# Hybrid block on one core: the second third's token tiles turned between the first block's products, four slots for the gated recurrence's results, and a later mark for the attention's first loads

## The chip, the cores and the metric

The kernel runs on 1 core of a Trainium2 chip. The metric is the device time of one execution in microseconds (us); less is better. The time before is the median of three runs. A profiled execution, taken apart from those runs, gives the trace.

## The reference

`reference.py` computes one layer of a streaming encoder on x (1 x 2048 x 1024, float32), with 16 learned meta tokens put ahead of the 2048 (T = 2064 tokens) and dropped at the end. Cut to what matters:

```python
h = concat(meta, x)
p = rms_norm(h, g_pre) @ W_in               # 1024 -> 512 + 1544 + 1024 columns, three head groups
a = rg_lru(p_a)                             # conv of 4 taps, gates, h_t = a_t h_(t-1) + b_t, times gelu(y); width 256
b = forgetting_attention(p_b)               # 8 heads of 64, causal softmax(q k / 8 + c_i - c_j) v, c = cumsum(log sigmoid(f))
c = rwkv7(p_c)                              # 4 heads of 64, state S_t = S (diag(w) - kk (kk a)^T) + v k^T, o_t = S_t r_t
h = h + rms_norm(concat(a, b, c) @ W_out, g_post)
g, v = causal_dwconv3(rms_norm(h, f_pre) @ W_up)      # 1024 -> 2 x 2816
h = h + rms_norm((gelu(g) * v) @ W_down, f_post)
```

The attention's f is 8 columns of p, one forget gate for each head.

## The kernel before, in words

**Products.** Each float32 operand is split into a rounded high part and the rest (xh, xl for tokens, wh, wl for weights), and a product is three matmuls: high by high, low by high, high by low (`mm3`, and L193 to L195 in the input projection). The tile names in the profile follow that: `psp` is the PSUM tile of an input column, `psf` that of the forget gate, `pst` that of a transpose.

**The input projection** runs in three thirds ("parts") of the tokens, and each part in two blocks of 128-token tiles: tiles 0 to 3 and 4 to 6, 7 to 9 and 10 to 12, 13 and 14, 15 and 16. Blocks are 400 and 384, 384 and 384, 256 and 256 tokens long. `w_in_norm` (L207) takes a part's tiles: it loads a tile (`token_load`), takes the mean square on ACT (L124), the power on POOL (L128) and scales on DVE (L148); then PE turns it in two halves of four 128x128 transposes (L161, `pst`), ACT writes the high part (L167) and DVE the low part (L168, `xl`). `norm_transpose` takes a tile from `core.held` if one lies there, and loads it otherwise. `w_in_part` then makes the forget gate (`w_in_gate`: L335 on xh, L336 on xl) and 24 weight columns of 128 ("c" for RWKV, "a" for the gated recurrence, k, v, q), each on both blocks. In part 0 the weights come from the input, are split and kept in DRAM (scr_wk); in parts 1 and 2 wh and wl are loaded from there (L260). In part 0 the second block's tiles are left unturned at first and are turned after the first two columns' products on the first block; the two columns' weights are loaded ahead. In parts 1 and 2 all tiles are turned, then the gate is made on both blocks, then the columns follow.

**Beside it.** A list of generators, `Beside`, is advanced 1.25 steps for each step of the projection. It holds `recurrences`: the forget gate's sums, the RWKV recurrence in blocks of 256 tokens (three for each part) and, behind each, `lru_block`, the gated recurrence (RG-LRU) on the same 256 tokens. The RWKV block makes its pair products on PE (L1232 from rwrav and rwbk, L1237, in PSUM tiles `rps`), masks them on DVE (L1241), sends triangles through DRAM (L1255, L1260), inverts them row by row on DVE (MEMSET L1282, L1288 over rwia and rwitmp), and then runs small 32x32 products on PE (L1317) with DVE steps between (L1340, L1347). `lru_block` works in two halves of 128 rows: a load of its input from DRAM (L1550, rwlraw), the first step on ACT (L1557, into the tile rwlu), three on DVE (L1559), two products for the gates, L1567 to L1591 on DVE and ACT, and the store of rwlu (L1592, to scr_mix). The tile rwlu has two slots: the third half waits until the first half's store has read its slot.

**The order of the work** on an engine is the order in which the program issues it, with some instructions held behind a named other one (`issue_after`) and the pools' slots deciding what waits. Each engine runs its queue in order. The attention (`Attn.run`) begins when the projection's last part is nearly done: the loads of its first heads' k and q (L605, L632) are placed in SP's queue behind `core.settled`, and its first memsets on DVE behind `core.parted`. Both marks are set in the main loop when the count of the last part's columns reaches `SETTLED` = 17. SP issues nearly all DMAs of the kernel, in order.

The rest of the kernel is the attention, W_out, and the feed-forward network (`psu`, `uw`, `psd`), most of the span; the diff does not touch it.

Of the kernel before, what the change touches and what calls it, by code (L numbers as in the profile page):

```python
# [18 lines left out]
P = 128  # L19
D = 1024  # L20
KD = D // P
META = 16
# [185 lines left out]
def w_in_norm(core, pools, psum, x, meta, gain, part):  # L208
    blocks = []
    for b, tl in enumerate(w_in_tokens(part)):  # L210
        t0 = tl[0][0]
        n = sum(r for _, r in tl)
        hi = pools["xn"].tile([P, KD, n], F32R, tag=f"xh{b}", name=core.n("xh"))
        apart = b == 1 and part < 2
        lo = pools["x1" if apart else "xn"].tile([P, KD, n], F32R, tag=f"xl{b}", name=core.n("xl"))
        blocks.append((t0, n, tl, hi, lo))

    def tile(block, s, rows):
        t0, _, _, hi, lo = block
        src = meta if s < META else x[s - META : s - META + rows, :]  # L220
        late = part == 1 and (s, rows) not in blocks[0][2][:2]
        after = (lambda: core.tc.issue_after(core.rounded.ins)) if late else nullcontext
        norm_transpose(core, pools, psum, src, rows, gain, [(hi, lo, s - t0, 0, rows)], after)

    core.unturned = []
    for block in blocks:
        for s, rows in block[2]:
            if part == 0 and block is blocks[1]:
                core.unturned.append((block, s, rows))
            else:  # L230
                tile(block, s, rows)
    core.turn_tile = lambda: tile(*core.unturned.pop(0))
    return blocks


def w_in_kept(scr, c0):

    return scr["wk"][c0 // P]
# [76 lines left out]
def w_in_gate(core, pools, psum, w_in, blocks, scr, part):  # L315

    nc = core.nc
    c0 = 2048
    home, tag = ("w", "wh") if part else ("us", "us")
    w = pools[home].tile([P, KD, P], F32R, tag=tag, name=core.n("fw"))  # L320
    flat, kept = w[:].rearrange("p k c -> p (k c)").bitcast(F32), w_in_kept(scr, 3 * D)[0]
    if part == 0:
        raw = pools["st"].tile([P, KD, 8], F32, tag="stv", name=core.n("fraw"))
        nc.sync.dma_start(raw[:], w_in[:, c0 : c0 + 8].rearrange("(k p) c -> p k c", p=P))
        nc.vector.memset(w[:].bitcast(F32), 0.0)
        nc.scalar.activation(w[:, :, 0:8], raw[:], AF.Copy)
        nc.vector.tensor_tensor(w[:, :, 32:40], raw[:], w[:, :, 0:8], op=ALU.subtract)
        nc.sync.dma_start(kept, flat)
    else:
        nc.sync.dma_start(flat, kept)  # L330

    def products(t0, n, tl, hi, lo):
        ps = psum.tile([P, 512], F32, tag="mm", name=core.n("psf"))
        for k in range(KD):
            nc.tensor.matmul(ps[:, :n], w[:, k], hi[:, k], start=k == 0, stop=False)  # L335
            nc.tensor.matmul(ps[:, :n], w[:, k], lo[:, k], start=False, stop=k == KD - 1)  # L336
        a = pools["st"].tile([8, 400], F32, tag="sth", name=core.n("fa"))
        nc.scalar.activation(a[:, :n], ps[32:40, :n], AF.Copy)
        o = pools["st"].tile([8, 400], F32, tag="stl", name=core.n("fo"))
        nc.vector.tensor_tensor(o[:, :n], ps[0:8, :n], a[:, :n], op=ALU.add)  # L340
        nc.sync.dma_start(scr["f"][:, t0 : t0 + n], o[:, :n])

    return products


def w_in_part(core, pools, psum, w_in, blocks, scr, part):
    gate = w_in_gate(core, pools, psum, w_in, blocks, scr, part)
    units = [("c", 2056 + P * i) for i in range(8)] + [("a", P * i) for i in range(4)]
    units += [(s, c + P * i) for s, c in (("k", 1024), ("v", 1536), ("q", 512)) for i in range(4)]
    waiting = [None]  # L350

    def step(*args):

        after = w_in_step(core, pools, psum, *args, scr)
        if waiting[0]:
            waiting[0]()
        waiting[0] = after

    if part == 0:
        raws = pools["rp"].tile([P, 2, KD, P], F32, tag="rw_e", name=core.n("raw"))  # L360
        firsts = [
            (w_in_weights(core, pools, w_in, c0, scr, part, raws[:, i], i > 0), kind, c0)
            for i, (kind, c0) in enumerate(units[:2])
        ]
        for i, block in enumerate(blocks):
            gate(*block)
            yield i > 0
            for w, kind, c0 in firsts:
                step(w, block, kind, c0)
                if i == 0:  # L370
                    core.turn_tile()
                yield i > 0
            while core.unturned:
                core.turn_tile()
        del units[:2]
    else:
        for block in blocks:
            gate(*block)
        yield False
        yield True  # L380

    for kind, c0 in units[:-2]:
        w = w_in_weights(core, pools, w_in, c0, scr, part)
        for block in blocks:
            step(w, block, kind, c0)
            yield block is blocks[-1]

    last = [(w_in_weights(core, pools, w_in, c0, scr, part), kind, c0) for kind, c0 in units[-2:]]
    for block in blocks:
        for w, kind, c0 in last:  # L390
            step(w, block, kind, c0)
            yield kind == "q" and c0 == last[-1][2]
# [1143 lines left out]
def lru_block(core, R, scr, k, b):  # L1536

    nc = core.nc
    t0 = max(0, Rwkv.start(b))
    n = min(T, Rwkv.start(b + 1)) - t0  # L1540
    c0 = PAD + t0
    tt = nc.vector.tensor_tensor
    stt = nc.vector.scalar_tensor_tensor

    def tl(s):
        return R.t([P, 256], s, bufs=2 if s == "lu" else 1)[:, :n]

    def raw(row, a):
        t = R.t([P, 260], "lraw", bufs=2)[:, : c0 + n - a]
        nc.sync.dma_start(t, scr["p"][row : row + P, a : c0 + n])  # L1550
        return t

    for p in range(2):
        pc = slice(p, p + 1)
        x = raw(P * p, c0 - 3)
        u, r, g, al = (tl("l" + s) for s in ("u", "r", "g", "a"))
        nc.scalar.activation(u, x[:, 3:], AF.Identity, scale=k["conv_w"][:, 6 + p : 7 + p], bias=k["conv_b"][:, pc])  # L1557
        for i in range(3):
            stt(u, x[:, i : n + i], k["conv_w"][:, 2 * i + p : 2 * i + p + 1], u, op0=ALU.mult, op1=ALU.add)  # L1559


        ps = R.pe()
        pa, px = ps[:, :n], ps[:, 256 : 256 + n]
        nc.tensor.matmul(pa, k["ga_w"][:, p], u, start=True, stop=True)
        nc.tensor.matmul(px, k["gx_w"][:, p], u, start=True, stop=True)
        nc.scalar.activation(r, pa, AF.Abs, bias=k["ga_b"][:, pc])
        nc.vector.tensor_scalar(al, pa, k["ga_b"][:, pc], 0.0, op0=ALU.add, op1=ALU.min)  # L1567
        nc.scalar.activation(g, px, AF.Tanh, scale=0.5, bias=k["rate"][:, 2, pc])
        nc.scalar.activation(r, r, AF.Tanh, scale=0.5)
        nc.scalar.activation(al, al, AF.Exp)  # L1570
        stt(r, r, 1.0, al, op0=ALU.add, op1=ALU.mult)
        stt(g, g, 1.0, u, op0=ALU.add, op1=ALU.mult)
        yield
        nc.scalar.activation(al, r, AF.Exp, scale=k["rate"][:, 0, pc])
        nc.scalar.activation(r, r, AF.Tanh, scale=k["rate"][:, 1, pc])

        tt(u, al, al, op=ALU.mult)
        stt(r, u, 1.0, r, op0=ALU.add, op1=ALU.mult)
        nc.vector.tensor_scalar(r, r, 1e-34, None, op0=ALU.max)
        nc.scalar.activation(r, r, AF.Sqrt)  # L1580
        stt(g, g, 0.5, r, op0=ALU.mult, op1=ALU.mult)
        nc.vector.tensor_tensor_scan(u, al, g, k["h"][:, pc], op0=ALU.mult, op1=ALU.add)
        nc.vector.tensor_copy(k["h"][:, pc], u[:, n - 1 : n])

        ya, y = raw(2 * P + P * p, c0), r
        nc.scalar.activation(y, ya, AF.Square)
        nc.vector.tensor_scalar(y, y, 0.044715, 1.0, op0=ALU.mult, op1=ALU.add)
        tt(y, y, ya, op=ALU.mult)
        nc.scalar.activation(y, y, AF.Tanh, scale=0.7978845608028654)
        stt(y, y, 1.0, ya, op0=ALU.add, op1=ALU.mult)  # L1590
        stt(u, u, 0.5, y, op0=ALU.mult, op1=ALU.mult)  # L1591
        nc.sync.dma_start(scr["mix"][P * p : P * p + P, t0 : t0 + n], u)  # L1592
        yield
# [558 lines left out]


READY = 13
SETTLED = 17
PACE = 1.25

WIDE = (0, 5)
# [379 lines left out]
```

## Time and profile before

| what | value |
|---|---|
| three runs, us | 2938.65, 2940.53, 2941.93 |
| median, us | 2940.53 |
| profiled execution, us | 2949.89 |
| its span, us | 2948.2 |
| PE busy | 96% of the span, 18854 matmuls |
| PEld (weight loads, beside PE) | 83% |
| DVE, ACT, POOL busy | 68%, 51%, 44% |
| mean granted clock of PE | 0.979 |
| DMA, mean over the span | 180 GB/s |

The page of the profile gives the busy time of each engine (PE: TensorE's matmuls, PEld: its weight loads, DVE: VectorE, ACT: ScalarE, POOL: GpSimd; SPq is the queue of SyncE, which issues DMAs) and the span in 40 slices of 73.7 us, with the clock that PE was granted in tenths. The other views are answers from the trace: a timeline lists instructions by start, with the idle time ahead of them and what ended it in brackets; a table of windows gives the busy time and granted clock between two points; the list of waits groups the idle time of an engine by what released it. A line number L1232 is that of the kernel before.

### The profile page before, as it was taken

To read this page: it belongs to the slowest core of one execution; us is meant where nothing else is said; L and a number is where in the kernel's file an instruction comes from. 1 tells how busy PE (TensorE), PEld (TensorE's weight loads), DVE (VectorE), ACT (ScalarE), POOL (GpSimd) and SP (SyncE) were. 2 spreads that over 40 slices of the span, in tenths; PEclk is the share of its full clock that TensorE was granted. 3 is DMA by queue.
4 is the path that set the end of the run, shared out by engine and by line. 5 is a ranking of instruction groups with operands and counts; after the bars stand their busy time and mean duration, and the time that the engine had idled before them with its cause. 6 is when DMAs were issued, how large, how long until landed. Compare 5 with 4: busy or idle time off the path is not lost.

```text
span 2948.2 us, 53211 instructions
## 1 busy us (share of the span) xinstructions
PE 2844.4 (96%) x18854; PEld 2446.0 (83%) x18854; DVE 2006.8 (68%) x3839; ACT 1502.3 (51%) x2937; POOL 1297.5 (44%) x1572
## 2 busy tenths in 40 slices
PE   8999999999988889999999999999999999999998
PEld 8998989888965555666578999999999999787887
DVE  4357655665678875556656988887777787556766
ACT  3246452454436654545645656666666665324333
POOL 1001222222114667677624676456655444656443
PEclk9998999999978999999999999999999999999999
DMA  7775678577643348444264665577777765436453
GB/s 241 250 245 185 215 240 291 174 241 246 204 120 77 90 115 227 97 122 129 48 192 148 212 194 179 160 233 209 219 199 222 215 198 149 141 111 218 151 170 122
DMA packets 470343, 530.51 MB, mean 180 GB/s; under 512 B 86862, under 2 KB 356888, under 8 KB 468524
## 3 DMA queue, kind: packets, MB, share of 16 engines
q1 hardware_dynamic: 469308, 526.18, 59.1%
q8 instruction: 148, 2.42, 0.4%
q0 software_dynamic: 768, 0.93, 0.1%
q14 instruction: 119, 0.97, 0.1%
HBM read 368.07 MB, written 158.90 MB: 179 GB/s over the span
## 4 chain that ended last, share of the span: by engine, by line
PE 75%; DVE 8%; DMA 6%; ACT 5%; issue 3%; POOL 2%; SPq 1%; DVEq 0%; POOLq 0%; ACTq 0%
PE psu L193 9%; PE psu L194 9%; PE psu L195 9%; PE psp L194 4%; PE psp L195 4%; PE psp L193 4%; PE psd L193 4%; PE psd L194 4%; PE psd L195 4%; PE po L797 4%; PE sc L774 2%; PE mx L645 2%; PE pswo L193 2%; PE pswo L194 2%; PE pswo L195 2%
## 5 line engine op out<-in xcount | busy, mean ns | idle before, releaser
L194 PE MATMUL psu<-xo,uw 128*128 128x344 f32 x1848 | 591.5, 320 | 0.0
L193 PE MATMUL psu<-xo,uw 128*128 128x344 f32 x1848 | 586.4, 322 | 3.0 <-DVE vb L1972 2.1
L195 PE MATMUL psu<-xo,uw 128*128 128x344 f32 x1848 | 581.9, 320 | 0.4 <-DVE uw L1781 0.3
L193 PE MATMUL psp<-xh,wh 128*128 128x384 f32 (+2 forms) x1152 | 380.4, 330 | 0.5 <-DMA wh<-scr_wk 0.5
L194 PE MATMUL psp<-xl,wh 128*128 128x384 f32 (+2 forms) x1152 | 375.3, 326 | 0.0
L195 PE MATMUL psp<-xh,wl 128*128 128x384 f32 (+2 forms) x1152 | 373.9, 325 | 0.4 <-DMA wl<-scr_wk 0.4
L1781 DVE TENSOR_TENSOR uw<-uq,uw 128x512 fp32r<-128x512 f32 x341 | 318.2, 938 | 62.5 <-ACT uw L1780 56.5
L193 PEld LDWEIGHTS psu<-xo,uw 128*128 128x128 f32 x1848 | 345.9, 188 | 5.2 <-DVE vb L1972 3.7
L194 PEld LDWEIGHTS psu<-xo,uw 128*128 128x128 f32 x1848 | 347.2, 188 | 0.0
L195 PEld LDWEIGHTS psu<-xo,uw 128*128 128x128 f32 x1848 | 345.7, 188 | 1.1 <-DVE uw L1781 1.1
L1780 ACT ACTIVATE uw<-uq 128x512 fp32r<-128x512 f32 x462 | 287.9, 627 | 95.2 <-PE psu L195 42.0
L779 ACT ACTIVATE p<-sc,bias 128x512 f32<-128x512 f32 (+4 forms) x352 | 197.6, 590 | 168.5 <-PE sc L775 147.5
L650 DVE TENSOR_REDUCE mc<-mx 128x1 f32<-128x512 f32 (+5 forms) x352 | 190.8, 566 | 110.4 <-PE mx L645 78.1
L1920 DVE SCALAR_TENSOR_TENSOR uy<-psu,ffn_cols,uy 128x342 f32<-128x342 f32 (+1 forms) x390 | 220.5, 567 | 61.9 <-ACT uy L1918 60.4
L1928 POOL TENSOR_TENSOR uy<-uy,uy 128x342 f32<-128x342 f32 (+1 forms) x132 | 145.4, 1102 | 231.5 <-ACT uw L1780 56.6
L1781 POOL TENSOR_TENSOR uw<-uq,uw 128x512 fp32r<-128x512 f32 x121 | 183.6, 1518 | 131.9 <-ACT uw L1780 108.8
L193 PEld LDWEIGHTS psp<-xh,wh 128*128 128x128 f32 x1152 | 218.9, 190 | 6.4 <-issue 3.7
L194 PEld LDWEIGHTS psp<-xl,wh 128*128 128x128 f32 x1152 | 219.0, 190 | 5.6 <-issue 4.0
L195 PEld LDWEIGHTS psp<-xh,wl 128*128 128x128 f32 x1152 | 218.9, 190 | 4.9 <-issue 2.9
L818 POOL TENSOR_TENSOR acc<-acc,p 128x512 f32<-128x512 f32 (+3 forms) x186 | 196.1, 1057 | 56.3 <-DVE acc L818 26.8
L1781 DVE TENSOR_TENSOR fo<-u,fo 128x896 fp32r<-128x896 f32 x88 | 100.6, 1143 | 131.0 <-ACT fo L1780 130.5
L1780 ACT ACTIVATE fo<-u 128x896 fp32r<-128x896 f32 x88 | 81.2, 923 | 206.7 <-PE psd L195 118.8
(492 smaller groups left out, 6309.8 us busy)
## 6 DMA issues: line engine op xcount, KB each, us to landing
uq<-scr_us SPq DMA_DIRECT2D x220, 256.0 KB
uq<-in_ffn_up_dram SPq DMA_DIRECT2D x209, 256.0 KB
wh<-scr_wk SPq DMA_DIRECT2D x48, 512.0 KB
wl<-scr_wk SPq DMA_DIRECT2D x48, 512.0 KB
u<-scr_ff SPq DMA_DIRECT2D x88, 256.0 KB
scr_ff<-uy SPq DMA_DIRECT2D x110, 171.0 KB
raw<-in_w_in_dram SPq DMA_DIRECT2D x24, 512.0 KB
scr_wk<-wh SPq DMA_DIRECT2D x24, 512.0 KB
```

The source lines that it names most:

```text
L193: nc.tensor.matmul(out, ah, bh, start=first, stop=False, skip_group_check=more)
L194: nc.tensor.matmul(out, ah, bl, start=False, stop=False, skip_group_check=more)
L195: nc.tensor.matmul(out, al, bh, start=False, stop=last, skip_group_check=more)
L645: nc.tensor.matmul(ps[:rows, : e - a], q3[:, qo : qo + rows], k2[:, a:e], start=True, stop=not last)
L650: self.reduced = nc.vector.tensor_reduce(mc[:rows, i, ci : ci + 1], ps[:rows, : e - a], axis=AX.X, op=ALU.max)
L779: last = nc.scalar.activation(p[:rows, :w], ps[:rows, :w], AF.Exp, bias=bias[:rows, j : j + 1])
L797: mm = nc.tensor.matmul(po[at : at + 64, c0:n], v1[:rows, j], p[:rows, : n - c0], start=start and i < 2, stop=end and i + 2 >= len(group), ...
L818: eng.tensor_tensor(a, ps_[0][0][:rows, c0:n] if start and i == 1 else a, p[:rows, : n - c0], op=ALU.add)
L1780: core.nc.scalar.activation(hi, src, AF.Copy)
L1781: (eng or core.nc.vector).tensor_tensor(lo, src, hi, op=ALU.subtract)
L1920: core.conved = stt(y[:, :n], src[:, i : n + i], cw[:, 44 * i + cc : 44 * i + cc + 1], y[:, :n], op0=ALU.mult, op1=ALU.add)
L1928: core.pooled = nc.gpsimd.tensor_tensor(v[:, :n], g[:, :n], v[:, :n], op=ALU.mult)
```

## The change

It has three parts.

- *The second third's tiles.* In part 1, as in part 0 before, only the first block's three tiles are turned ahead; the second block's three tiles are loaded (into `core.held`) and are turned one by one between the products of the first two columns on the first block: one after each of these products, the last after both. The first two columns' weights are loaded ahead of the gate in part 1 too. The gate's weights of part 1 go to the `us` pool, as in part 0, and not to one of the two `wh` slots.
- *The gated recurrence's results.* The tile rwlu has four slots and not two.
- *The attention's first loads.* `SETTLED` is 21 and not 17: the loads of the first heads' k and q, and the attention's memsets, are placed four columns later.

```diff
@@ -222,13 +222,13 @@ def w_in_norm
-    core.unturned = []
-    for block in blocks:
-        for s, rows in block[2]:
-            if part == 0 and block is blocks[1]:
-                core.unturned.append((block, s, rows))
-            else:
-                tile(block, s, rows)
+    core.unturned = [(blocks[1], s, rows) for s, rows in blocks[1][2] if part < 2]
+    for s, rows in blocks[0][2]:
+        tile(blocks[0], s, rows)
+    if part == 1:
+        core.held = [token_load(core, pools, x[s - META : s - META + rows, :], rows) for _, s, rows in core.unturned]
+    for s, rows in blocks[1][2] if part == 2 else ():
+        tile(blocks[1], s, rows)
     core.turn_tile = lambda: tile(*core.unturned.pop(0))
@@ -316,7 +316,7 @@ def w_in_gate
-    home, tag = ("w", "wh") if part else ("us", "us")
+    home, tag = ("w", "wh") if part == 2 else ("us", "us")
@@ -358,8 +358,9 @@ def w_in_part
     if part == 0:
         raws = pools["rp"].tile([P, 2, KD, P], F32, tag="rw_e", name=core.n("raw"))
+    if part < 2:
         firsts = [
-            (w_in_weights(core, pools, w_in, c0, scr, part, raws[:, i], i > 0), kind, c0)
+            (w_in_weights(core, pools, w_in, c0, scr, part, *((raws[:, i], i > 0) if part == 0 else ())), kind, c0)
             for i, (kind, c0) in enumerate(units[:2])
         ]
@@ -367,7 +368,7 @@ def w_in_part
                 step(w, block, kind, c0)
-                if i == 0:
+                if core.unturned:
                     core.turn_tile()
@@ -1543,7 +1544,7 @@ def lru_block
-        return R.t([P, 256], s, bufs=2 if s == "lu" else 1)[:, :n]
+        return R.t([P, 256], s, bufs=4 if s == "lu" else 1)[:, :n]
@@ -2152,7 +2153,7 @@
-SETTLED = 17
+SETTLED = 21
```

The added line `if part < 2:` makes every line number behind it one higher in the change: L1232 is L1233 there, L1282 is L1283, and so on.

Three places in the engines' orders show what moved. The first is PE's order where the first third passes to the second. Before, the last of the second third's transposes (pst) come around the RWKV recurrence's pair products (rps) and then the gate (psf):

```order
L1178 MATMUL eps_2058<-ident,rwe_1982 128x128 x4
L161 MATMUL pst_3133<-ident,xt_3118 128x128
L161 MATMUL pst_3148<-ident,xt_3140 128x128 x4
L161 MATMUL pst_3155<-ident,xt_3140 128x128 x4
L161 MATMUL pst_3170<-ident,xt_3162 128x128 x4
L161 MATMUL pst_3177<-ident,xt_3162 128x128 x4
L1232 MATMUL rps_2138<-rwrav_2079,rwbk_2086 128x128
L1237 MATMUL rps_2139<-rwrav_2079,rwbk_2086 64x128 x2
...
L1209 MATMUL eps_2096<-rwsq_1994,bones 128x512
L161 MATMUL pst_3192<-ident,xt_3184 128x128 x4
...
L335 MATMUL psf_3230<-xh_3092,fw_3228 128x384
L336 MATMUL psf_3230<-xl_3093,fw_3228 128x384
```

The same place in the change, where psp_3293 is the first weight column on block 0 and xt_3140 block 0's last tile:

```order
L1179 MATMUL eps_2058<-ident,rwe_1982 128x128 x4
L161 MATMUL pst_3133<-ident,xt_3118 128x128 x2
L161 MATMUL pst_3148<-ident,xt_3140 128x128 x4
L161 MATMUL pst_3155<-ident,xt_3140 128x128 x4
L335 MATMUL psf_3178<-xh_3092,fw_3168 128x384
L336 MATMUL psf_3178<-xl_3093,fw_3168 128x384
...
L193 MATMUL psp_3293<-xh_3092,wh_3170 128x384
L194 MATMUL psp_3293<-xl_3093,wh_3170 128x384
L161 MATMUL pst_3327<-ident,xt_3162 128x128 x4
L161 MATMUL pst_3334<-ident,xt_3162 128x128 x4
```

The gate and the first column on block 0 have moved ahead of the pair products and of the second block's transposes.

The second is DVE's order a little later, around the recurrence's triangular inverse (rwia, rwitmp). Before, the low parts of the second block's last tiles (xl_3095) come ahead of the gated recurrence's steps (rwla, rwlg) and of the memset of the inverse:

```order
L168 TENSOR_TENSOR xl_3095<-pst_3214,xh_3094 128x4x128
L168 TENSOR_TENSOR xl_3095<-pst_3221,xh_3094 128x4x128
L1241 TENSOR_TENSOR rwsc_2136<-rps_2154,rmask 128x4x128
L1241 TENSOR_TENSOR rwsc_2136<-rps_2155,rmask 128x4x128
L1262 TENSOR_TENSOR rwbk_2086<-rwbk_2086,rwwc_2091 128x1024
L1567 TENSOR_SCALAR rwla_2928<-eps_2933,lru_cols 128x256
...
L1581 SCALAR_TENSOR_TENSOR rwlg_2927<-rwlg_2927,rwlr_2926 128x256
L1282 MEMSET rwia_2222 128x16
L1582 SCALAR_TENSOR_TENSOR rwlu_2925<-rwla_2928,lru_h,rwlg_2927 128x256
L1288 TENSOR_REDUCE rwix_2258<-rwitmp_2261 128x8
```

In the change, the rows around the same memset (L1283 there):

```order
L1592 SCALAR_TENSOR_TENSOR rwlu_2925<-rwlu_2925,rwlr_2926 128x256
L1283 MEMSET rwia_2222 128x16
L1289 TENSOR_REDUCE rwix_2258<-rwitmp_2261 128x8 x2
L168 TENSOR_TENSOR xl_3095<-pst_3409,xh_3094 128x4x128
L1289 TENSOR_REDUCE rwix_2258<-rwitmp_2261 128x8
L168 TENSOR_TENSOR xl_3095<-pst_3416,xh_3094 128x4x128
L1568 TENSOR_SCALAR rwla_3028<-eps_3033,lru_cols 128x256
L1289 TENSOR_REDUCE rwix_2258<-rwitmp_2261 128x8
L168 TENSOR_TENSOR xl_3095<-pst_3475,xh_3094 128x4x128
L168 TENSOR_TENSOR xl_3095<-pst_3482,xh_3094 128x4x128
```

The last four low parts have moved behind the memset, and steps of the inverse stand among them.

The third is SP's order late in the projection. Before, the attention's first loads (k, q) stand among the loads of the gated recurrence's input (rwlraw) and the store of its result (rwlu):

```order
L1805 DMA us_8822<-in_ffn_up_dram 128x2x128 x3
L605 DMA k_1402_11222<-scr_kh 64x1040
L632 DMA q_1404_11231<-scr_qh 64x512
L1550 DMA rwlraw_9576<-scr_p 128x256
L289 DMA scr_p<-stp_8355 128x256
L632 DMA q_1405_11235<-scr_qh 64x512
L605 DMA k_1402_11222<-scr_kh 64x1040
L632 DMA q_1403_11227<-scr_qh 64x512
L1550 DMA rwlraw_9626<-scr_p 128x259
L1592 DMA scr_mix<-rwlu_8192 128x256
```

In the change:

```order
L1806 DMA us_8822<-in_ffn_up_dram 128x2x128 x3
L1551 DMA rwlraw_9576<-scr_p 128x256
L289 DMA scr_p<-stp_8355 128x256
L1551 DMA rwlraw_9626<-scr_p 128x259
L1593 DMA scr_mix<-rwlu_8192 128x256
```

The five loads have moved further back in SP's queue.

## The prediction

> **What bounds the kernel now.** I read the page first, then the granted clock in windows of 20 us and of 1 us, then the PE timeline wherever one of these showed a hole, then the queues of the engines that PE waited for there.
>
> The page, parts 1 and 2:
>
> ```profile
> PE 2844.4 (96%) x18854; PEld 2446.0 (83%) x18854; DVE 2006.8 (68%) x3839; ACT 1502.3 (51%) x2937; POOL 1297.5 (44%) x1572
> ...
> PE   8999999999988889999999999999999999999998
> ...
> PEclk9998999999978999999999999999999999999999
> ```
>
> PE is the bound; time can be won only where it idles or where its clock was halved. The fourth slice of PEclk and the stretch of 8s at 850 to 1110 us show where.
>
> Six windows (columns: length, then busy us and count of PE, PEld, DVE, ACT, POOL, then PEclk, DMA share, GB/s):
>
> ```profile
> 267.64:280.98 13.34, 11.08 (x44) 7.62 (x44) 12.31 (x21) 5.73 (x13) 5.39 (x6) 0.50 0.68 223
> 284.28:287.58 3.30, 3.30 (x13) 2.90 (x10) 2.70 (x4) 1.07 (x3) 0.00 (x0) 0.52 0.10 11
> 288.00:291.80 3.80, 3.80 (x23) 3.80 (x22) 2.23 (x6) 1.57 (x4) 0.00 (x0) 1.00 0.11 12
> 625.88:629.20 3.32, 3.32 (x13) 2.96 (x13) 2.52 (x10) 2.77 (x5) 1.92 (x4) 0.50 1.06 363
> 728.40:738.20 9.80, 9.43 (x91) 8.71 (x91) 4.23 (x13) 2.73 (x6) 0.47 (x1) 0.50 0.67 220
> 854.00:888.00 34.00, 28.82 (x112) 19.92 (x114) 22.96 (x62) 12.52 (x29) 6.52 (x12) 0.51 0.64 148
> ```
>
> At a clock of 0.50 half of the busy time is lost: 5.5 + 1.6 = 7.1 us where the first third passes to the second, 4.7 us at 728, 14 us at 854. The third row is the full-speed rate: 23 matmuls in 3.80 us, 0.17 us each.
>
> PE's timeline (start, duration, line, tile, count, and in brackets the idle time before it with its releaser):
>
> ```profile
> 259.48 1.80 PE L161 MATMUL pst<-ident,xt 128*128 128x128 f32 x15
> ...
> 269.90 0.79 PE L1232 MATMUL rps<-rwrav,rwbk 64*128 64x128 f32 x2 [5.66 <-DVE rwbk L1200]
> ...
> 275.26 2.07 PE L1209 MATMUL eps<-rwsq,bones 128*128 128x512 f32 x2
> ...
> 281.21 0.48 PE L1232 MATMUL rps<-rwrav,rwbk 64*128 64x128 f32 x2
> ...
> 281.62 0.43 PE L1237 MATMUL rps<-rwrav,rwbk 64*64 64x128 f32 x4
> ...
> 281.99 0.48 PE L1232 MATMUL rps<-rwrav,rwbk 64*128 64x128 f32 x2
> ...
> 624.54 0.75 PE L1317 MATMUL rps<-rwxu,rwsc 32*32 32x32 f32 x64 [1.70 <-ACT rwsc L1270]
> ...
> 728.77 0.31 PE L1317 MATMUL rps<-rwxf,rwxu 32*32 32x32 f32 x2 [4.08 <-DVE rwxu L1347]
> ```
>
> A transpose costs 0.12 us, one L1232/L1237 pair 0.78 us at full clock. The holes of 5.66 and 4.08 us are each followed by the slow clock; even 1.70 us with 32x32 matmuls behind it brought one slow window.
>
> **The change part by part.** The sum is made against the profiled execution, 2949.89 us (span 2948.2). The three timed runs have a median of 2940.53, 9.4 us less; the same difference is applied to that. 0.2% is 5.9 us, about what a measurement of this kernel can tell from no change: faster means below 2934.6, slower above 2946.4.
>
> *First hole (259 to 294).* On PE, before, four of the second third's six tiles are transposed ahead of the first L1232 (L1233 in the change, whose line numbers are one higher from 361 on) and two behind it, before the gate. In the change, by the order shown above, the transposes of block 0, the gate and the first products on block 0 come first, and L1233 behind them. PE now waits for the low parts of block 0 instead of for rwbk. DVE's timeline from there:
>
> ```profile
> 261.65 1.87 DVE L168 TENSOR_TENSOR xl<-pst,xh 128x512 fp32r<-128x512 f32 x3
> ...
> 263.45 0.86 DVE L1190 SCALAR_TENSOR_TENSOR rwk<-rwk,rwkv_cols,eps 128x256 f32<-128x256 f32 x2
> ...
> 264.23 0.68 DVE L1198 TENSOR_TENSOR rwrav<-rwr,rwe 128x512 f32<-128x512 f32 x1
> ...
> 266.10 0.68 DVE L1192 SCALAR_TENSOR_TENSOR rwe<-rwe,rwk 128x512 f32<-128x512 f32 x1
> ```
>
> L336 needs the fifth L168 (third tile, first half). In the changed DVE order five L168 (0.61 each, 3.1), the two of L1190 (0.8) and three 512-column steps (0.68 less the 0.07 by which such rows overlap, 0.6 each, 1.8) come up to and with it: 261.65 + 5.7 = 267.4. PE has its 24 transposes and four L1178 (0.5) done at 259.48 + 3.4 = 262.9 and one L335 in between: idle 4.3 instead of 5.66, **−1.3**. The hole stays long enough for the slow clock. But gate, psp and transposes that use the whole array now follow, 7 us of them at half rate, where before the half-height L1232/L1237 came: one or two windows of 3.3 us, 1.7 to 3.3 lost, say 2.4, against 7.1: **−4.7**. The gate's weights come from a buffer free since the first third, so both wh buffers are free for the first two columns; that load's 0.5 MB at 30 to 40 us, and the first columns' arrival behind two token loads, I cost at 0 (a load takes 5 us, below, and PE reaches them 7 us after the last product); uncovered it is 0 to 2.
>
> *A new wait (294 to 300).* The last two tiles' transposes stand behind the first two columns on block 0. On DVE every L168 (xl, the low parts) stood ahead of MEMSET L1282, before; in the change the four of these two tiles stand behind it, with steps of the recurrence's triangular inverse (rwia, rwitmp: its rows return from DRAM) among them. What that MEMSET waits for, at this place and at 610 us:
>
> ```profile
> 284.07 1.29 DVE L1241 TENSOR_TENSOR rwsc<-rps,rmask 128x512 f32<-128x512 f32 x2 [1.97 <-PE rps L1232]
> ...
> 284.79 3.65 SPq L1255 DMA_DIRECT2D da<-rwsc  x8
> ...
> 296.68 0.17 DVE L1288 TENSOR_REDUCE rwix<-rwitmp 128x8 f32<-128x16 f32 x1
> ...
> 297.44 0.16 DVE L1288 TENSOR_REDUCE rwix<-rwitmp 128x8 f32<-128x24 f32 x1
> ...
> 612.78 1.87 SPq L1255 DMA_DIRECT2D da<-rwsc  x4
> ...
> 615.88 1.14 SPq L1260 DMA_DIRECT2D rwia<-da  x2
> ...
> 618.75 0.07 DVE L1282 MEMSET rwia<- 128x16 f32 x1 [4.45 <-DMA rwia<-da]
> ```
>
> From L1241's first half on: 0.7, eight issues 3.65, 1.2 until L1260 (614.65 to 615.88), 2.9 until the MEMSET may run: 8.4 us. In the change PE does, from 267.4 to the end of its second L1232 group, 35 gate and psp (6.0), 8 transposes (1.0), 8 pairs (6.2), L1209 (2.07 at half clock, 1.0) and the gated recurrence's two small products (estimated as much, 1.0), 15.2, plus the 1.7 to 3.3 of slow clock: 284.3 to 285.9, no earlier than now. So the MEMSET runs at 292.7 to 294.3; two L1288 steps follow (0.9 and 0.8 by their spacing), then three L168, one L1567 and two L1288 (2.7): the gate's first low product on block 1 at 297.1 to 298.7. PE reaches it 28 psp (4.8), 16 identity products (1.8), 16 transposes (1.9), the small products (1.0) and three matmuls (0.5) after that group, 10.0: 294.3 to 295.9. A wait of 2.8, **+2.8**; nothing stands behind it on PE that could run, in order as it is. From 0, should the DMA be back sooner, to 5. The slow clock may follow (1.7 to 3.3) or not: **+1.2**.
>
> *Four result slots and later loads (713 to 738).* The waits list has all of ACT's waits for a result's store; the rest is the worst of the six (SPq: DMA issues):
>
> ```profile
> ACT rwlu L1557 <- DMA scr_mix<-rwlu: 16.2, 6, 8.2
> 708.55 0.43 SPq L1550 DMA_DIRECT2D rwlraw<-scr_p  x1
> ...
> 713.69 0.60 ACT L1557 ACTIVATE rwlu<-rwlraw,lru_cols 128x256 f32<-128x256 f32 x1 [0.67 <-DMA rwlraw<-scr_p]
> ...
> 721.67 0.53 SPq L1550 DMA_DIRECT2D rwlraw<-scr_p  x1
> ...
> 722.51 0.33 SPq L1592 DMA_DIRECT2D scr_mix<-rwlu  x1
> ...
> 722.95 1.72 DVE L1340 TENSOR_TENSOR rwxf<-rps,rwxu 32x256 f32<-32x256 f32 x4
> ...
> 724.70 0.42 DVE L60 COPY stp<-psp 128x256 f32<-128x256 f32 x1
> ...
> 726.96 0.60 ACT L1557 ACTIVATE rwlu<-rwlraw,lru_cols 128x256 f32<-128x256 f32 x1 [8.18 <-DMA scr_mix<-rwlu]
> ...
> 727.60 0.48 DVE L1559 SCALAR_TENSOR_TENSOR rwlu<-rwlraw,lru_cols,rwlu 128x256 f32<-128x256 f32 x1 [2.17 <-ACT rwlu L1557]
> ...
> 728.30 0.88 DVE L1347 COPY rwxu<-rps 32x256 f32<-32x256 f32 x2
> ```
>
> ACT waits 8.18 us for a store issued at 722.51; DVE's L1559 waits for ACT, L1347 stands behind L1559, and PE's 4.08 us end with L1347. With four slots only the input is needed. In the change, the attention's five loads (k, q) are gone from ahead of the input, which is issued five issues of 0.53 and a little between them, some 3 us, sooner, at 718.5; with 5.1 us to land as at 708.55 it is there at 723.6 at the latest, before DVE needs it. DVE then runs on from 725.1 through L1559, L1288, L1559 (0.4, 0.2, 0.4) and half of L1347 (0.4): PE goes on at 726.6, not 728.77: **−2.1**. About 2 us of idle and the 32x32 products remain, as at 624.54; that the 4.7 us of slow clock go is even odds: **−2.4**. The other five waits on a store have no hole of PE beside them: 0. The loads moved later are wanted by the attention at about 850 (the sixth window), some 80 us after their new place, four columns on: 0, or up to 2 if they fall among its own.
>
> Sum: −1.3 − 4.7 + 2.8 + 1.2 − 2.1 − 2.4 = −6.5: 2943.4 for the profiled execution, **2934.0** for the median. What follows up to 1110 us keeps its work but in another mixture; taken as 0, with −6 (somewhat under half of the 14 us lost at 854) to +14 (as much again) as bounds.
>
> **A rule weighed.** The row of 625.88 shows the clock halved after 1.70 us of idle, and that of 267.64 shows it halved for four windows although PE was busy for 11.08 of 13.34 us. The Trainium skill (TensorE: Matmul & The Clock Gate, Part 1) says that the clock halves after an idle window of about 3.4 us and comes back after one busy window. Both rows disagree with that here, so I don't sum by it; it would make the sum the first rival's.
>
> **The rivals.** *The clock falls only after a hole as long as those of 5.66 and 4.08, and one window restores it, as in the rows of 284.28 and 625.88*: then 1.7 is lost at the first hole (−5.4), nothing at the new wait, and all 4.7 is won at 728: −1.3 − 5.4 + 2.8 − 2.1 − 4.7 = −10.7, 2929.8. Against it: the row of 624.54. By the Trainium skill's rule the same. 0.15.
>
> *The new wait does not come*, because the inverse's rows are back before PE is there: −10.5, 2930. Its bound by the 610 us rows speaks against it. 0.10.
>
> *No gain arrives*: the recurrence's chain, not PE, sets when the attention can run, and what PE wins it waits for at 850; in the change the last products run ahead of the recurrence: by its order 49 rather than 92 of them stand between the same two recurrence products ahead of the attention's first. For it: PE is at 0.85 of 34 us there. 2940.5. 0.18.
>
> *The attention starts worse*: more of the recurrence's chain of small products then stands beside it, each waiting for DVE, and the slow stretch of 854 lasts as long again. It decides if over half of that comes: +14 − 6.5 = +7.5, 2948. For it: that stretch has been slow for 34 us already, on holes of 2 to 3 us. Against it: its work is the same. 0.16.
>
> The change does put the tiles, slots and loads where it says, by the order; that it doesn't is no case.
>
> **How the numbers follow.** The forecast has 0.41, its own range is 2930 to 2939; two thirds of it lie below 2934.6. Faster: 0.27 + 0.15 + 0.10 = 0.52, rounded down to 0.51 for the second rival's upper end. Slower: 0.14 of the last rival. Same: the rest, 0.35. The range takes in the third rival whole, the low rivals with a little of the later stage's −6 (2922), and the last one up to 2947.
>
> **What would show it.** Right: an idle of 3.5 to 4.5 us before an L336 near 267, the clock back at full by 275; a wait of 2 to 4 us before a gate product near 297 with DVE L168 as its releaser, behind MEMSET L1283; no wait of ACT's L1558 on scr_mix; the hole near 720 to 728 halved. Wrong: the first hole gone or followed by 13 us of slow clock again; L168 of block 1 done before the MEMSET; a changed slow stretch at the attention's start that is larger than all of these.

## The result and the profile after

The change is slower: 2948.57 us, the median of 22 runs (2940.39 to 2959.38), against 2941.86 us for the kernel before, run 22 times beside it (2934.57 to 2956.53). The ratio is 1.0025, with an interval of 1.0014 to 1.0036, so some 7 us more. Two later runs of the same kernel gave 1.0028 (1.0016 to 1.0041) and 1.0049 (1.0030 to 1.0068).

Single executions of one kernel spread over some 20 us, and a profile shows one execution. The profiled one of before (2949.89 us) is among its longer ones, the first profiled one of the change (2940.39 us) is the shortest of 22. Two spans alone would tell the wrong sign here. So stages are compared below over several profiles: four executions of the change were profiled (spans 2938.7, 2945.3, 2957.7 and 2942.7 us).

The page of the first profile after, parts 1 and 2, for the lines shown of before:

```profile
PE 2828.0 (96%) x18854; PEld 2437.4 (83%) x18854; DVE 2002.6 (68%) x3839; ACT 1500.8 (51%) x2937; POOL 1301.8 (44%) x1572
...
PEclk9999999999979999999999999999999999999999
```

The slow slice at 221 to 295 us is gone from PEclk; the one at 850 us is still there.

PE's timeline at the first passage (start, duration, line, tile, count, idle before it and its releaser):

```profile
264.20 0.45 PE L335 MATMUL psf<-xh,fw 128*128 128x384 f32 x1 [0.60 <-DVE rwk L1191]
267.90 0.44 PE L336 MATMUL psf<-xl,fw 128*128 128x384 f32 x1 [3.26 <-DVE xl L168]
...
273.39 0.49 PE L1233 MATMUL rps<-rwrav,rwbk 64*128 64x128 f32 x2
...
295.63 0.44 PE L335 MATMUL psf<-xh,fw 128*128 128x384 f32 x1 [1.31 <-ACT xh L167]
...
296.79 0.44 PE L336 MATMUL psf<-xl,fw 128*128 128x384 f32 x1 [0.37 <-DVE xl L168]
```

The holes are 0.60 + 3.26 us, not 5.66, and the second ends with L168 at 267.90. The windows of the same profile (columns as in the prediction):

```profile
269.12:272.53 3.41, 3.41 (x15) 3.13 (x14) 3.40 (x7) 1.91 (x6) 1.49 (x2) 0.50 1.03 420
294.32:296.40 2.08, 0.77 (x3) 0.47 (x3) 2.08 (x7) 2.08 (x5) 0.74 (x3) 1.00 0.00 1
```

One window of 3.41 us at half clock follows the hole, where before there were 16.6 us of it. At the second place PE idles 1.3 of 2.08 us, and 0.37 us more before L336 at 296.79. DVE's timeline there:

```profile
293.15 0.07 DVE L1283 MEMSET rwia<- 128x16 f32 x1 [0.98 <-DMA rwia<-da]
...
294.27 0.69 DVE L168 TENSOR_TENSOR xl<-pst,xh 128x512 fp32r<-128x512 f32 x1
...
296.06 1.27 DVE L168 TENSOR_TENSOR xl<-pst,xh 128x512 fp32r<-128x512 f32 x2
```

The four L168 do stand behind the memset, which ran at 293.15 us.

Around 728 us, the windows from 700 to 745 us of before and of the change, one row each:

```profile
700.00:745.00 45.00, 39.56 (x528) 36.88 (x528) 25.10 (x72) 21.29 (x48) 16.48 (x28) 0.89 0.74 219
```

```profile
700.00:745.00 45.00, 42.58 (x620) 39.20 (x619) 27.00 (x80) 22.69 (x54) 14.56 (x26) 1.00 0.71 227
```

PE did 92 more matmuls in the same 45 us, at full clock. Of the hole of 4.08 us, 0.57 is left:

```profile
722.18 0.24 PE L1318 MATMUL rps<-rwxf,rwxu 32*32 32x32 f32 x2 [0.57 <-DVE rwxu L1348]
```

ACT waits for no store of rwlu any more; what is left of L1558's waits is its input:

```profile
ACT rwlu L1558 <- DMA rwlraw<-scr_p: 19.7, 9, 4.6
```

So both holes named in the prediction shrank, and the new wait is shorter than forecast. The time is lost behind the last weight column. Windows from the last product of a column to the first of W_out: before, and then, with the stretch ahead of it, the change's third profile (span 2957.7 us, an execution of 2959.45 us):

```profile
845.90:1157.40 311.50, 273.51 (x2230) 174.06 (x2229) 226.96 (x594) 172.91 (x370) 173.25 (x261) 0.88 0.50 129
```

```profile
0.00:836.10 836.10, 799.26 (x7035) 740.37 (x7035) 487.93 (x1219) 372.70 (x741) 155.02 (x268) 0.98 0.70 226
...
836.10:1166.30 330.20, 275.98 (x2306) 176.24 (x2305) 235.76 (x609) 175.27 (x375) 173.63 (x263) 0.87 0.48 121
```

The change has its columns done at 836.1 us, 9.8 us sooner than before, and then needs 330 us and not 311 us to reach W_out. In its other three profiles the columns end at 836.1, 836.0 and 837.6 us, and this stage takes 312, 320 and 314 us. What follows W_out's first product is the same in both within 2 us. Before was profiled once, in an execution 8 us above the median of its 22; if its spread is made in this stage, as that of the change is (last section), a usual execution of before takes some 303 us here, an estimate.

Why the stage is longer was not settled by these two traces; the experiments were made for that.

### The profile page after: what moved, and what is told of

Its sections match the earlier page's. It is cut to its first block, busy times and chain, and to the rows that moved or that the text cites. A ratio compares the mean times of both kernels' runs of the same rounds, so it can differ in the third digit from the quotient of the medians.

```text
span 2938.7 us, 53187 instructions
## 1 busy us (share of the span) xinstructions
PE 2828.0 (96%) x18854; PEld 2437.4 (83%) x18854; DVE 2002.6 (68%) x3839; ACT 1500.8 (51%) x2937; POOL 1301.8 (44%) x1572
## 4 chain that ended last, share of the span: by engine, by line
PE 72%; DVE 9%; DMA 6%; ACT 5%; issue 3%; POOL 3%; SPq 1%; DVEq 0%; POOLq 0%; ACTq 0%
PE psu L193 9%; PE psu L194 9%; PE psu L195 9%; PE po L798 4%; PE psd L193 4%; PE psd L194 4%; PE psd L195 4%; PE psp L193 4%; PE psp L195 4%; PE psp L194 4%; PE sc L775 2%; PE pswo L193 2%; PE pswo L194 2%; PE pswo L195 2%; PE mx L646 2%
```

## The experiments

The theories at the start: *(T)* the tiles cost, *(S)* the slots cost, *(L)* loads marked late reach the attention late, *(O)* the order on PE at the attention's start costs, by how the recurrence's rest lies among the attention's products. All times against the kernel before are ratios from runs on the same chip.

**Each part alone, and two together.** The tiles alone (the change with `bufs=2` and `SETTLED = 17`):

> Only the second third's tiles are turned between the first block's products; two result slots, mark at 17. By my sum of the four terms of the first passage (-1.3, -4.7, +2.8, +1.2) it is 2 us faster than the kernel before. If this part is what makes the change slower (it runs the recurrence beside other columns for the whole second third, so that its work stands in another place at every later hole), it is 5 us slower or more. If the cost lies in the later mark or in the slots, it is within 3 us of before.

1.0029 (1.0014 to 1.0043), slower by 8.6 us by the medians. Against my sum. The hole at 728 us is back, a row of PE's timeline in this kernel:

```profile
726.73 0.31 PE L1318 MATMUL rps<-rwxf,rwxu 32*32 32x32 f32 x2 [3.94 <-DVE rwxu L1348]
```

The slots alone:

```diff
-        return R.t([P, 256], s, bufs=2 if s == "lu" else 1)[:, :n]
+        return R.t([P, 256], s, bufs=4 if s == "lu" else 1)[:, :n]
```

> Only the four result slots. By my account the input of the fifth block's second half is then the last to arrive at 727 us, behind the attention's loads in SP's queue: hardly a gain, 0 to -2 us. If the slots let the gated recurrence run ahead and its steps then stand before the RWKV recurrence's on ACT and DVE, it is slower, by 3 us or more.

0.9992 (0.9978 to 1.0006). The hole of PE is halved with this alone, and the half-clock time there is mostly gone (granted clock 0.96 from 700 to 745 us, where before has 0.89):

```profile
732.69 0.24 PE L1317 MATMUL rps<-rwxf,rwxu 32*32 32x32 f32 x2 [2.04 <-DVE rwxu L1347]
```

What is left is the input, which comes last, as expected: in the list of ACT's waits of this kernel the stores are gone, and the longest wait for the input, 6.6 us, ends inside this hole, at 730.88 us:

```profile
ACT rwlu L1557 <- DMA rwlraw<-scr_p: 20.6, 10, 6.6
```

S falls.

The mark alone (`SETTLED = 21` in the kernel before):

> Only the mark of the attention's first loads and memsets at 21. By my account nothing is lost at the attention's start, and the store at 722 us leaves SP some 3 us sooner: 0 to -3 us. If the later loads reach the attention too late, or fall among its own, it is slower by 5 us or more, and PE waits at the first scores for a load of q or k.

0.9994 (0.9981 to 1.0006). From 700 to 745 us its granted clock is 0.99 and PE is busy for 42.0 us: the five loads out of SP's way were enough by themselves, although ACT still waits for the store here, 3.5 us and no longer 8.2. As the expectation's first branch; the hole in this kernel:

```profile
725.05 0.24 PE L1317 MATMUL rps<-rwxf,rwxu 32*32 32x32 f32 x2 [0.47 <-DVE rwxu L1347]
```

Tiles and slots, with the mark at 17:

> The change without the later mark. If the mark is what costs, it is at least 5 us faster than the whole change, so no slower than before. If the tiles or the slots cost, it stays about 7 us slower than before, like the whole change. By my sum: 2 to 4 us faster than before.

0.9992 (0.9978 to 1.0007), 2.7 us less by the medians. So what made tiles alone slow is not there with four slots, and the mark, harmless alone, made the change slow. The hole at 728 us is not what made them slow, for it is here too, with ACT waiting 8.4 us for its input:

```profile
729.90 0.24 PE L1318 MATMUL rps<-rwxf,rwxu 32*32 32x32 f32 x2 [3.92 <-DVE rwxu L1348]
```

The parts don't add up: 1.0029, 0.9992 and 0.9994 alone, 0.9992 for two, 1.0025 for all three. That speaks for something that all three move, which is O.

**Late loads or order.** The change once more, then three kernels in which loads and order part ways:

> The change once more, beside the next three on one chip, and with another profile. Both theories: 5 to 9 us slower than the kernel before. If its profile is a usual one, the time is lost between the last weight column (846 us before) and the end of the recurrence (about 1120), by 6 us or more against the 311 us of before; ahead of that it is no later than before.

1.0028 (1.0016 to 1.0041). Its profile, again the shortest of its executions, loses 9 us more in the stage than before; ahead of it it is 10 us sooner.

The change with only the loads late, the memsets at 17:

```diff
-                    if part == 2 and i == SETTLED:
-                        core.settled, core.parted = core.loaded.ins, core.split.ins
+                    if part == 2 and i == 21:
+                        core.settled = core.loaded.ins
+                    if part == 2 and i == 17:
+                        core.parted = core.split.ins
```

> The change, but only the loads of k and q have the later mark (21); the attention's memsets keep theirs (17). PE's order behind the attention's first product is then that of before but for 8 rows, and the loads are as late as in the change. If late loads are what costs: 5 to 9 us slower than before. If the order of PE's work in the attention's first 270 us is what costs: 1 to 5 us faster than before, like the tiles and slots without the mark.

0.9992 (0.9979 to 1.0004), like tiles and slots without the mark: L falls, O stands. The traces bear it out: at the attention's first scores PE waits for a load of q 2.0 to 2.6 us in the change's four profiles, and 2.2 us in before; before, then the change's first profile:

```profile
853.94 0.66 PE L774 MATMUL sc<-q,k 128*128 128x512 f32 x2 [2.18 <-DMA q<-scr_qh]
```

```profile
850.16 1.10 PE L775 MATMUL sc<-q,k 128*128 128x512 f32 x2 [1.99 <-DMA q<-scr_qh]
```

The same with 21 and 17 exchanged (only the memsets late):

> The change, but only the memsets have the later mark (21); the loads keep theirs (17). The recurrence's rest stands further back among the attention's products: its first hundreds of rps behind 119, 144, 206 and 304 products of the attention, like the change's 125, 152, 206 and 304, where before has 88, 114, 169 and 282. If late loads cost: 1 to 5 us faster than before. If the order costs: 4 to 9 us slower.

1.0005 (0.9993 to 1.0017): between the two branches, some 4 us over the run before it. It is neither the change's loss nor the gain. From the change it differs by the loads' mark alone, and it is 7 us faster by the medians; that mark moves PE's order as well (the table below has both), so how much is the order's was not told apart here.

The kernel before with `SETTLED = 16`:

> The kernel before with the mark at 16, one column earlier: neither the tiles nor the slots, and no load later than before. The recurrence's rest stands behind 119, 144, 206, 304, 347 and 522 products of the attention, as in the run before this one. If late loads cost: within 2 us of before. If the order costs: 5 to 10 us slower than before.

0.9995 (0.9984 to 1.0006). Here O, as I had put it, was wrong: the recurrence's hundreds stand behind nearly as many attention products as in the change, and it costs nothing. The count that matters had to be another one (below).

**The order put back.** The change with `SETTLED = 22`: every load and memset later still, PE's order behind the attention's first product that of before but for 8 rows.

> The change with the mark at 22 and not 21: the loads and the memsets come one column later still. PE's order behind the attention's first product is that of before but for 8 rows. If a late mark costs by itself: 6 to 10 us slower than before, like the change or worse. If PE's order at the attention's start costs: 1 to 5 us faster than before.

0.9971 (0.9952 to 0.9990), and with the run below 0.9978 (0.9967 to 0.9990). Nothing that the change adds is taken out, and by these ratios it is 6 to 9 us faster than before. Of the things that were told apart, only the order on PE (and on the engines that go with it) is left for the change's loss. Its median granted clock over the runs is 0.9835, where before has 0.981 and the change 0.9805 and 0.979: 0.0025 of 2940 us is 7 us, lost in some 15 us at half clock.

**The wait for the third keys.** All four profiles of the change have a wait of 7.4 to 8.5 us that before has with 2.1 us; the row in the list of waits of before, of the change's first profile and of its third:

```profile
PE mx L645 <- DMA k<-scr_cl: 2.1, 1, 2.1
```

```profile
PE mx L646 <- DMA k<-scr_cl: 7.5, 1, 7.5
```

```profile
PE mx L646 <- DMA k<-scr_cl: 8.5, 1, 8.5
```

The load stands behind the recurrence's last store in SP's queue. That store, moved to POOL's:

```diff
-        nc.sync.dma_start(
+        (nc.gpsimd if b == 8 else nc.sync).dma_start(
             self.scr["mix"][768:1024, t0 : t0 + n - a].rearrange("(p r) t -> r p t", r=P), fo[:, :, a:n]
```

> The change, with the RWKV recurrence's last store moved from SP's queue to POOL's; PE's order as in the change but for 12 rows. In both profiles of the change PE waits 7.5 us for k<-scr_cl near 1080 us, which stands behind that store in SP's queue; SP waits some 2 us there for the store. If the store's wait sets the hole: the hole shrinks by 2 us, and the time by 2 to 4 us against the change (3 to 7 us slower than before). If the hole comes from SP's whole order standing behind PE's: the hole stays over 6 us, and the time at 6 to 9 us above before.

1.0015 (0.9999 to 1.0031), and the hole is 5.4 us: the first branch, by 2 us of hole and about 3 us of time (the intervals of this and of the change overlap). What holds the load now, from the list of SP's waits between 1060 and 1092 us and from DVE's timeline in this kernel:

```profile
SPq L608 <- DVE k L568: 2.4, 1, 2.4
SPq L606 <- PE rps L1474: 1.7, 1, 1.7
```

```profile
1081.54 0.22 DVE L1482 TENSOR_TENSOR rwxu<-rwxu,rps 128x64 f32<-128x64 f32 x1
1081.79 2.81 DVE L568 CAST k<-ident 64x520 fp32r<-64x520 f32 x4
```

L606 waits for the recurrence's last product (L1474) and L568 follows its last DVE step (L1482) at once: the third key tile lies in memory that the recurrence holds to its end. So the attention's second half can't start before the recurrence has ended, wherever the store is.

**The tiles alone in another order** (`bufs=2`, `SETTLED = 22`):

> Only the tiles, with the mark at 22: another order behind the attention's first product (the recurrence's hundreds behind 88, 113, 158, 271, 306 and 466 products of the attention; the tiles alone with the mark at 17 have 88, 113, 153, 242, 279 and 414, before has 88, 114, 169, 282, 329 and 494). If the tiles themselves cost, it is 6 us or more slower than before, as the tiles alone were. If the order they came with cost, it is within 4 us of before.

1.0052 (1.0033 to 1.0072). Slower in this order too. By the expectation the tiles themselves cost with two slots; but this order isn't before's either, and no version of the tiles with two slots and before's order was found. That stays open.

**Side by side.** The change and the mark at 22 on one chip, and a fourth profile of the change:

> The change beside the same with the mark at 22, on one chip. Both earlier profiles of the change were its fastest executions. If the cost is the order at the attention's start, this kernel is 6 us or more slower than the next one, and a usual execution's profile loses it between the last weight column and the first product of W_out (846 to 1157 us before), in more slow clock and in a wait of over 5 us for k<-scr_cl; in the other stages it is within 3 us of the next kernel.

> The change with the mark at 22 once more. If the first run of it told the truth, it is 3 to 10 us faster than the kernel before and faster than the change on the same chip by 6 us or more. If that run was luck, it is within 2 us of before.

> One more profile of the change, for a usual execution: the wait for k<-scr_cl near 1080 us is over 5 us in it as in the other two, and the time is lost in the attention's start, not ahead of it.

1.0049 (1.0030 to 1.0068) for the change, 0.9978 (0.9967 to 0.9990) for the mark at 22: the version with the mark at 22 beats both kernels. The change's third profile is of a usual execution (2959.45 us, its median here 2960.01). The fourth is not: with 2944.42 us it is as fast as the median of before beside it (2944.32), though its wait for the third keys is 7.4 us. Two rows of the version with the mark at 22, to be held against those of the change above:

```profile
0.00:844.90 844.90, 806.74 (x7111) 745.71 (x7111) 490.06 (x1232) 375.14 (x745) 154.61 (x269) 0.98 0.69 224
...
844.90:1143.10 298.20, 263.93 (x2230) 168.79 (x2229) 226.77 (x594) 172.51 (x370) 172.28 (x260) 0.91 0.52 134
```

Its columns end 8.8 us later than the change's (the expectation had the other stages within 3 us), and it is at W_out 23.2 us sooner: 32 us between the two in one stage, 12 of them busy time of PE (275.98 against 263.93, at the lower clock and with 76 matmuls more) and 20 idle.

Where this comes from is seen in the place of one step: the last pair products (L1238) of the recurrence's last full block, behind which only a short block follows. First with the mark at 22, then in the change:

```profile
875.99 1.09 PE L1238 MATMUL rps<-rwrav,rwbk 64*64 64x128 f32 x16
```

```profile
891.98 1.97 PE L1238 MATMUL rps<-rwrav,rwbk 64*64 64x128 f32 x16
```

16 us later, although the columns were done 8.8 us sooner. Its end is 20.7 us later in these two profiles. With the mark at 22:

```profile
1063.74 0.33 PE L1474 MATMUL rps<-rwsg,g_up 128*128 128x64 f32 x2
...
1072.08 0.77 PE L646 MATMUL mx<-k,q 128*128 128x400 f32 x3 [1.81 <-DMA k<-scr_cl]
```

In the change:

```profile
1084.41 0.69 PE L1474 MATMUL rps<-rwsg,g_up 128*128 128x64 f32 x2
...
1094.57 1.31 PE L646 MATMUL mx<-k,q 128*128 128x400 f32 x3 [8.51 <-DMA k<-scr_cl]
```

Both have the second half's first product 8 to 10 us behind L1474; only, in the change PE is idle for 8.51 us of it.

Counted in the traces, for every profile (column products still to do behind the recurrence's L1394 near 839 us; attention products, that is mx, sc and po, ahead of the last full block's last row of L1238, and where that row starts; line numbers of the change; times in us):

| kernel | last column | column products left at L1394 | attention products ahead of that L1238 | at | last L1474 | first of W_out | ratio |
|---|---|---|---|---|---|---|---|
| before | 845.9 | 26 | 50 | 882 | 1077.9 | 1157.4 | 1 |
| slots | 847.4 | 28 | 50 | 884 | 1070.7 | 1148.9 | 0.9992 |
| tiles, slots | 844.7 | 28 | 50 | 882 | 1069.6 | 1149.6 | 0.9992 |
| loads late | 846.8 | 27 | 50 | 878 | 1063.5 | 1143.2 | 0.9992 |
| mark 22 | 846.4 | 21 | 50 | 883 | 1069.8 | 1148.9 | 0.9971 |
| mark 22 again | 844.9 | 21 | 50 | 876 | 1063.8 | 1143.1 | 0.9978 |
| before, mark 16 | 851.0 | 47 | 50 | 880 | 1072.0 | 1155.0 | 0.9995 |
| before, mark 21 | 845.1 | 9 | 98 | 887 | 1073.2 | 1156.1 | 0.9994 |
| memsets late | 847.6 | 11 | 77 | 887 | 1075.2 | 1155.0 | 1.0005 |
| the change | 836.1 | 0 | 110 | 890 | 1069.2 | 1148.2 | 1.0025 |
| the change again | 836.0 | 0 | 110 | 892 | 1077.1 | 1156.2 | 1.0028 |
| the change, third | 836.1 | 0 | 110 | 892 | 1084.7 | 1166.3 | 1.0049 |
| the change, fourth | 837.6 | 0 | 110 | 890 | 1070.9 | 1151.9 | |
| store on POOL | 839.1 | 0 | 110 | 893 | 1079.9 | 1156.6 | 1.0015 |
| tiles | 843.1 | 26 | 50 | 879 | 1066.4 | 1163.7 | 1.0029 |
| tiles, mark 22 | 848.9 | 25 | 50 | 880 | 1076.0 | 1161.4 | 1.0052 |

In the change all column products are used up before the recurrence's L1394, and 110 attention products, not 50, stand ahead of these pair products. From the last column to them the change's four profiles take 53 to 56 us, and the six profiles with before's order (the table's first six rows) 31 to 37; from there to the last L1474 they take 180 to 193 against 185 to 195, and from L1474 to W_out 79 to 82 against 78 to 80. So the loss is made ahead of the pair products, and the later steps of the recurrence do not make it up. The mark alone has 98 and isn't slower, so this count doesn't settle the loss either; it still had 9 column products left there. In the two kernels with tiles and two slots the count is 50 and the recurrence ends in time, but only 591 and 604 attention products are done ahead of its last L1474 (647 before, 664 in the change), and W_out starts 97 and 85 us behind it (80 before). Shown is that the loss lies in this stage, that it goes when the order goes back, and that in the change it is made ahead of the pair products. Behind L1474 the wait for the third keys takes back what the attention products done earlier would have saved there (79 to 82 us against 78 to 80, with 17 products fewer to do), and no more. Which row of the order costs how much was not told apart, nor why the mark at 22 does better than the mark at 17 (0.9971 and 0.9978 against 0.9992, whose intervals overlap).

## Why the prediction was wrong, point by point

*What bounds the kernel, and where time can be won.* Right: PE, and the holes with their slow clock. The versions with the order of before and with both tiles and slots were 3 to 10 us faster by their medians (2943.2, 2943.35, 2935.55, 2935.9 against 2945.87, 2946.32, 2945.85, 2944.32); for the first two of them the interval takes in no gain as well.

*The first hole, −1.3 and −4.7.* Right in mechanism and near in size: idle 3.86 instead of 5.66 us (−1.8), and one window at half clock instead of five (1.7 lost, not 7.1: −5.4). The hole ended at 267.90, by my sum at 267.4.

*The new wait, +2.8 and +1.2.* Right in place and sign, half in size. The memset ran at 293.15 us (292.7 to 294.3 by my sum), but PE was there no sooner than 294.3 us and lost 1.3 us, released by ACT's xh, and only 0.37 us more at L336 by the L168 that I had named; no slow clock followed.

*Given back within the second third.* Not foreseen. The terms as measured come to −5.5 (−1.8 − 5.4 + 1.3 + 0.4) and not −2.0. At the last column product of the second third, though, the four kernels without the tiles are at 590.8, 594.7, 587.2 and 588.1 us and the change's four profiles at 589.3, 584.4, 587.8 and 589.5 us: 2.4 us sooner in the mean, with single profiles of either kind 5 to 7 us apart. Part of what the passage won may have been work put off: the recurrence was left further behind, and PE waited for it at another place, where before had no hole (the change's first profile):

```profile
343.23 0.28 PE L1414 MATMUL rps<-rstate,rwgt 64*64 64x64 f32 x2 [3.26 <-DVE rstate L1418]
```

*Slots and loads, −2.1 and −2.4.* Right, and too small: 0.57 of the 4.08 us is left, and the slow clock went. The later loads did it: the mark alone leaves 0.47 us, the slots alone 2.04, tiles and slots 3.92. That the slots were needed too is not shown.

*"What follows up to 1110 us keeps its work but in another mixture; taken as 0".* This is the step that failed. The mixture cost more than all terms won: the stage from the last column to W_out took 312 to 330 us in the change and 298.2 and 302.5 us with the same parts and the mark at 22. The working had a bound of +14 for it, and the signs were there too: I had read in the order that 49 rather than 92 column products stand between two recurrence products, and took it for a rival of no gain. A column product that has moved ahead of the recurrence fills no wait of the recurrence later; attention products stand there instead, and in this order 60 more of them ran ahead of the last full block's pair products, which came 6 to 16 us later than with before's order, though the columns had ended 7 to 11 us sooner.

*The rivals.* The last one ("the attention starts worse", 0.16, 2948 us) is what came, at 2948.57 us; that the number fits to 0.6 us is luck, for the bound of +14 was not worked out from the order. Its mechanism was half right: the recurrence's chain stands beside the attention for longer (233 to 249 us from the last column to the last L1474, against 217 to 232). What it lacked is that the attention's second half waits for memory that the recurrence holds, so that a later end of the recurrence is a later start of that half. *No gain arrives* had the right engine of the loss (the recurrence's chain) and the wrong price. *The new wait does not come* came halfway. The first rival's clock fits the first hole of the change in part: one window restored the clock, but the hole that halved it was 3.26 us long, shorter than the two that this rival names. The Trainium skill (TensorE: Matmul & The Clock Gate, Part 1) has it that one busy window restores the clock; the row of 269.12 agrees, while the row of 267.64 of before does not.

*The numbers.* The range ended at 2947, 1.6 us short; the sum with the working's own bound of +14 was 2948. A stage whose bounds were −6 and +14 us outweighed a sum of −6.5 us, and its middle, +4, should have stood in the sum in the place of 0: with it the forecast would have been no change.

## What to carry to other kernels

When engines run fixed queues, a change early in the program moves the rows of every later stage; look in the new order at the stage with the longest chain of small steps, and count what filler is left beside that chain, before adding up what the holes in front of it are worth. Where one stage's buffers lie in memory that another stage frees at its end, the end of that stage is a start time for the next one, and moving work ahead of it bought nothing here. Where executions of one kernel spread by more than the effect, compare stages over several profiles, and trust no pair of spans.

## What the runs showed of the hardware that was not expected

The spread of the change's executions is made in one stage. In the four profiles of the change the last column ends at 836.0 to 837.6 us, within 1.6 us; W_out starts at 1148.2 to 1166.3 us, 18 us apart; and what follows takes the same time within 2.4 us. The work and its order are the same in all four. Half-clock stretches come in steps of 3.41 us (the row of 269.12:272.53 is one; in this stage of the third profile they are 3.4, 6.8, 13.7 and 20.5 us long), and this stage, with its many waits of up to 3 us, has 65 to 85 us of them.
